# Value products as whole blocks, and where the first weights of the up-projection are kept, in a decoder layer on one core

## The chip, the cores and the metric

The kernel runs on one core of one Trainium2 chip. The metric is the device time of one execution in microseconds, the median of several runs. A profiled execution gives the trace that is read here. In what follows PE is TensorE, PEld its weight loads, DVE is VectorE, ACT is ScalarE, POOL is GpSimd, and SP is the engine that issues most of the loads; a q behind a name (SPq, POOLq) is that engine's DMA queue.

## The reference, cut to what matters

One layer of a hybrid decoder over 512 tokens of width 1024, in float32: a state-space mixer and a forgetting attention (FoX, 16 heads of 64) on the same normalised input, an output projection, and a gated MLP with a short convolution.

```
x (1, 512, 1024)

def fox_mixer(q, k, v, f_raw, ...):
    ...
    for start in range(0, s, Q_BLOCK):          # blocks of 128 queries
        ...
        p = jax.nn.softmax(jnp.where(causal, logits, -jnp.inf), axis=-1)
        outs.append(jnp.einsum('bhqk,bhkd->bhqd', p.astype(vh.dtype), vh[:, :, :end]))
...
def conv_gated_mlp(x, w_up, conv_w, conv_b, w_down):
    h = x @ w_up.astype(x.dtype)                # 1024 -> 2 x 2816
    h = causal_depthwise_conv(h, conv_w, conv_b)
    gate, val = jnp.split(h, 2, axis=-1)
    return (jax.nn.silu(gate) * val) @ w_down.astype(x.dtype)
...
    h = rms_norm(x, norm_mix_w[layer])
    ...                                         # both mixers, from one projection of h
    x = x + (mixed @ w_out[layer].astype(mixed.dtype)).astype(x.dtype)
    hf = rms_norm(x, norm_ffn_w[layer])
    x = x + conv_gated_mlp(hf, ...)
```

## The kernel before

Every large product is made in three: each operand is split into a high part (a cast to a shorter form of float32) and a low part (what the cast left), and high x high, high x low and low x high are added up in PSUM (`mm3`, L107 to L113; its matmuls all have line L110). A weight block of 128x1024 is loaded as it is, ACT casts it (`wh`), DVE subtracts (`wl`). For the up-projection this is `split_up`, L921 to L924.

The stages follow one another on PE: projections and state-space scan to about 216 us, FoX attention with further projections between its pieces to about 421, the output projection (`po`) to 438.6, the up-projection to about 650, the down-projection to the end. A scheduler writes out one order for each engine from the program's order, from priorities (`urgent()` raises what is made in it) and from marks that put one instruction behind another (`issue_after`, `keep_in_program_order`); each engine then runs its own order, and an instruction that waits holds up what stands behind it on its engine.

*FoX.* The heads go in pairs. Queries and keys of later pairs are transposed (`qkT`, L601), logits S are made (L651, L652), softmax leaves `prob`; `fox_turn` (L663 to L677) transposes `prob` in 128x128 pieces (`pT`, L674) and ACT copies them to `pt` (L676). `fox_values` (L679 to L695) multiplies by v: eight matmuls for a pair, each two records in the trace, one head in the lower 64 output rows (LO) and one in the upper (HI), alternating. In the program they keep their order, but other instructions may come between them. Products of other projections (`pw`) fill PE in this stage.

*Start of the up-projection.* w_up is cut into blocks of eleven "quads", each with four quarters B11, B12, B21, B22. Quad 0 is made plainly (`plain`, L1271 to L1287): each quarter is loaded into a `wraw` tile, split, and multiplied with the two halves of the tokens; the sums are the PSUM tiles G and Z. Its weight pairs (`wh`, `wl`) come from a spare place for B12, and otherwise from a pool `wp` of three pairs, two of which hold the output projection's last weights (`w7`) until these have been used. The tokens are normalised in four blocks `tb` (`up_norm`, L845 to L855: ACT's square L847, DVE and POOL's power L125/L126, DVE's scaling L852), transposed on PE (`hT`, L864) and split by ACT and DVE (L867 to L879) into `uh`, `ul`, `ghl`. `up_sums` (L884 to L908) makes sums of token blocks for the later quads.

Quads 1 and on take seven products, n0 to n6, instead of eight. A tile Ta is loaded with B11 (`load_a`); n0's weights are split from it; then POOL's queue adds B12 onto it by a DMA that accumulates (`more`, L967 and L968), n2's weights are split from the sum, and so on. So a later addition must wait until both splits of the step before have read Ta. The Ta tiles are one in the pool `pu` (quads 1, 4, ...) and two in the pool `ptt` (the others). SP issues the plain loads in order (L972, L978, L1277).

Of the kernel before, what the change touches and what calls it, by code (L numbers as in the profile page):

```python
# [8 lines left out]
F32 = mybir.dt.float32  # L9
F32R = mybir.dt.float32r  # L10
# [5 lines left out]
P = 128  # L16
SEQ = 512
D = 1024
NK = D // P
NTB = SEQ // P  # L20
# [13 lines left out]
LINE = 64  # L34
# [5 lines left out]
def tile_hybrid_layer(  # L40
# [18 lines left out]
    nc = tc.nc  # L59
    act, dve, pool, pe = nc.scalar, nc.vector, nc.gpsimd, nc.tensor  # L60

    cp = ctx.enter_context(tc.tile_pool(name="cp", bufs=1))
    wp = ctx.enter_context(tc.tile_pool(name="wp", bufs=2))
# [11 lines left out]
    def raw(ap):  # L75
        return ap.bitcast(F32)
# [41 lines left out]
    def mbank(name="m"):  # L118
        return bank_pools["pm"].tile([P, 512], F32, tag="m", name=name)

    def obank(name="o"):
        return bank_pools["po"].tile([P, 512], F32, tag="o", name=name)
# [9 lines left out]
    def columns(n):  # L132
        taken_columns[0] += n
        return misc[:, taken_columns[0] - n : taken_columns[0]]
# [31 lines left out]
    r = columns(NTB)  # L166
# [59 lines left out]
    for k in range(NK):  # L226
        ins = pe.matmul(pdt[:64, :], wdt[:, k, :], xh[:, k, :], start=k == 0, stop=False, skip_group_check=True)
        if k < 2:
            tc.keep_in_program_order(ins)
            keep_busy(64 * (1 - k))  # L230
        ins = pe.matmul(
            pdt[:32, :], wdt[:, k, 0:32], xl[:, k, :], start=False, stop=k == NK - 1, skip_group_check=True
        )
# [72 lines left out]
    LO, HI = slice(0, HD), slice(HD, P)  # L306
# [150 lines left out]
    squares, copied = [], {}  # L457
# [205 lines left out]
    def fox_turn(prob):  # L663
        where = {}
        for n, kbs in enumerate(((2,), (1, 3), (0,))):
            w = sum(SEQ - kb * P for kb in kbs)
            t = mbank("pT")
            pt = pf.tile([P, w], F32, tag="pt%d" % n, name="pt", bufs=4 if n == 0 else 3)
            w = 0
            for kb in kbs:  # L670
                where[kb] = (pt, w)
                for qb in range(kb, NTB):
                    o = QOFF[qb] + kb * P
                    pe.transpose(t[:, w : w + P], prob[:, o : o + P], ident)  # L674
                    w += P
            act.copy(pt, t[:, :w])  # L676
        return where  # L677

    def fox_values(pair, turned, v):  # L679
        o = obank("o")  # L680
        for kb in range(NTB):
            for i, rows in ((1, HI), (0, LO)):
                pt, w = turned[i][kb]
                ins = pe.matmul(  # L684
                    o[rows, kb * P :], v[:, kb, (2 * pair + i) % 8, :], pt[:, w : w + SEQ - kb * P],
                    start=kb == 0, stop=kb == NTB - 1, skip_group_check=True,
                )
                if (kb, i) != (0, 1):
                    tc.keep_in_program_order(ins)
        values_last.append(ins)  # L690
        mh = pmf.tile([P, SEQ], F32R, tag="mfh", name="mfh", bufs=2)
        ml = pmf.tile([P, SEQ], F32R, tag="mfl", name="mfl", bufs=2)
        act.copy(mh, o)
        dve.tensor_sub(ml, o, raw(mh))
        return mh, ml  # L695

    def urgent():
        return tc.high_priority(AHEAD)
# [37 lines left out]
    turned = {}  # L736
# [61 lines left out]
    B11, B12, B21, B22 = 0, 1, 2, 3  # L798
    ADD, SUB = ALU.add, ALU.subtract

    ptt = ctx.enter_context(tc.tile_pool(name="ptt", bufs=1, side="right", reuse_waits="tile"))
# [3 lines left out]
    pu = pu_ctx.enter_context(tc.tile_pool(name="pu", bufs=1, side="right", reuse_waits="tile"))  # L805
# [10 lines left out]
    def up_operand(n):  # L816
        return (oh[:, n], ol[:, n]) if n < 4 else (sh[:, n - 4], sl[:, n - 4])
# [16 lines left out]
    def in_turn(engine, ins):  # L834
        if engine in turn_of:
            dep = mybir.DependencyInfo(mybir.DependencyClass.NoSync, mybir.DependencyReason.DATA)
            tc.add_manual_dep(ins.ins, turn_of[engine].ins.name, dep, reason="issue_after")
        turn_of[engine] = ins
        return ins
# [44 lines left out]
    def up_sums(tb):  # L884
        s = slice((tb % 2) * P, (tb % 2 + 1) * P)
        g1, k1, g2, k2, d1, d2 = [t[:, :, s] for t in (one[:, 0], one[:, 1], two[:, 0], two[:, 1], s1, s2)]
        turn_of.update(zip(("ACT", "DVE"), made_of[tb]))

        def sum_(dst, a, b, op):
            in_turn("DVE", op(dst, a, b))  # L890

        def parts(n, src):
            h, l = [t[:, :, s] for t in up_operand(n)]
            in_turn("ACT", act.copy(h, src))
            return lambda: in_turn("DVE", dve.tensor_sub(l, src, raw(h)))

        sum_(d1, g2, k2, dve.tensor_sub)
        low3 = parts(3, d1)
        sum_(d2, d1, g1, dve.tensor_sub)
        low4 = parts(4, d2)  # L900
        low3()
        sum_(k1, k1, d2, dve.tensor_add)
        low6 = parts(6, k1)
        low4()
        sum_(g2, g1, g2, dve.tensor_sub)
        low5 = parts(5, g2)
        low6()
        low5()  # L908
# [12 lines left out]
    def split_up(r, where=None):  # L921
        h, l = where or [wp.tile([P, 1024], F32R, tag=t, name=t, bufs=3) for t in ("wh", "wl")]
        ordered(act.copy(h, r), lambda: dve.tensor_tensor(out=l, in0=r, in1=raw(h), op=SUB))  # L923
        return h, l  # L924
# [5 lines left out]
    def pair(n):  # L930
        if FROM[n] not in pairs:
            return None
        pairs[n] = pairs.pop(FROM[n])
        return pairs[n]
# [7 lines left out]
    quads = [Quad() for _ in range(NH)]  # L942
    H1, H2 = slice(0, HT), slice(HT, SEQ)

    halfway, last_product, last_pool = [None], [None], [None]

    def product(w, n, o, part, first=False, last=True):
        h, l = w
        ah, al = up_operand(n) if n is not None else (gh, gl)
        for p in range(2):  # L950
            for k in range(4):
                c = slice(p * 512 + k * P, p * 512 + (k + 1) * P)
                ins = mm3(
                    o[:, p, part], h[:, c], l[:, c], ah[:, k], al[:, k], first and k == 0, last and k == 3, grouped=False
                )
            if p == 0:
                halfway[0] = ins
        last_product[0] = ins
# [6 lines left out]
    last_more = [None]  # L965

    def more(t, quarter, q):  # L967
        last_more[0] = nc.gpsimd.dma_start(t, wup[quarter, q], accum_op=ALU.add)  # L968
# [6 lines left out]
    def load_a(q):  # L975
        u = quads[q]
        u.ta = (pu if q % 3 == 1 else ptt).tile([P, 1024], F32, tag="T", name="Ta", bufs=1 if q % 3 == 1 else 2)
        nc.sync.dma_start(u.ta, wup[B11, q])  # L978

    def n0_weights(q, where=None):  # L980
        u = quads[q]
        if not hasattr(u, "ta"):
            load_a(q)
        u.w0 = split_up(u.ta, where or pair("n0"))
        u.at = made[0] - 1
        more(u.ta, B12, q)

    def n1_weights(q):
        u = quads[q]
# [34 lines left out]
    def n0(q, where=None):  # L1024
        if not hasattr(quads[q], "w0"):
            n0_weights(q, where)
        n0_product(q)
        with urgent():
            n0_kept(q)
# [167 lines left out]
    T = []  # L1197
# [70 lines left out]
    def spare():  # L1268
        return [pa.tile([P, 1024], F32R, tag=t, name=t, bufs=1) for t in ("wh", "wl")]

    def plain(q):  # L1271
        u = quads[q]
        u.ws, u.halfway = [], []

        def weights(quarter, where=None):
            r = wp.tile([P, 1024], F32, tag="wraw", name="wraw", bufs=3)
            nc.sync.dma_start(r, wup[quarter, q])  # L1277
            u.ws.append(split_up(r, where))

        def tokens(half):  # L1280
            for n, (name, rows) in enumerate((("Z", 0), ("Z", 1), ("G", 0), ("G", 1))):
                o = getattr(u, name)
                op = ((0, 1), (None, 2))[half][rows]
                product(u.ws[n], op, o, (H1, H2)[half], rows == 0, rows == 1)
                u.halfway.append(halfway[0])

        return weights, tokens  # L1287

    for tb in range(NTB):
        if tb == 2:  # L1290
            out_part(wa1[0], m1, 1, (2, 3), rs[1])
        if tb == NTB - 1:
            weights, tokens = plain(0)
# [9 lines left out]
    quads[0].Z = two_banks("Z", "Z")  # L1303
    sum_banks.close()
    up_banks["G"] = ctx.enter_context(tc.tile_pool(name="pq", bufs=2, space=PSUM, reuse_waits="tile"))
    weights(B11)
    with urgent():
        normed = up_norm(NTB - 1)
        act.activation(warm[:, 0:1], ss[:, NTB - 1 : NTB], AF.Silu)
# [7 lines left out]
    with urgent(), tc.issue_after(quads[0].halfway[1].ins):  # L1317
        up_turn(NTB - 1, hT3)
        up_sums(NTB - 1)
    tokens(1)  # L1320
    n0(1, spare())
    n1_weights(1)
# [1 line left out]
    n2(1)  # L1324
    n5(1)
    four = [[wp.tile([P, 1024], F32R, tag=t, name=t, bufs=3) for t in ("wh", "wl")] for _ in range(3)]

    four.append([pu.tile([P, 1024 + LINE], F32R, tag=t, name=t)[:, LINE // 4 : 1024 + LINE // 4] for t in ("wh", "wl")])
    pairs.update(n2=four[0], n4=four[3], n1=four[1], n5=four[2])
    n0_weights(2)  # L1330
    n3_weights(1)
# [19 lines left out]
    q = NH - 1  # L1351
# [277 lines left out]
```

## Time and profile before

| | |
|---|---|
| median of 3 runs | 768.64 us (767.77 to 768.9) |
| profiled execution, its own time | 770.09 us |
| its span | 768.3 us |
| busy: PE / DVE / ACT / POOL | 759.0 / 600.0 / 489.0 / 201.0 us |
| granted clock of PE | 1.00 |
| DMA moved | 112.39 MB, mean 146 GB/s |

The span is shorter than the execution's own time, which has what lies around it. Rows of the time line give start, length, engine, line, operation, output<-inputs and, in brackets, how long the engine had been idle and what ended that. Rows of the chain give start, length and what ran. Matmuls are pipelined, so rows overlap; the distance between the starts of two of them says what one costs.

### The profile page before, as it was taken

The numbers are of one execution on the slowest core, as the hardware profiler recorded it, in microseconds if no ns is written. First come the engines' busy times: TensorE is split into PE (matmuls) and PEld (weight loads), VectorE is DVE, ScalarE is ACT, GpSimd is POOL, SyncE is SP. The second block draws the span as 40 slices with busy tenths as digits, with TensorE's granted clock in tenths as the row PEclk, the third lists the DMA queues.
The fourth block names the chain that finished last, engine by engine and source line by source line (L and its number), as shares of the span: only waits on it lengthen the run. The fifth ranks groups of instructions, "written<-read, shape, count | busy, mean of one in ns | idle before, by whom it ended". The sixth has DMA issues, their size and how long they took to land.

```text
span 768.3 us, 12543 instructions
## 1 busy us (share of the span) xinstructions
PE 759.0 (99%) x4647; PEld 652.2 (85%) x4647; DVE 600.0 (78%) x965; ACT 489.0 (64%) x870; POOL 201.0 (26%) x250
## 2 busy tenths in 40 slices
PE   9999999999999999999999999999999999999997
PEld 7888878888888768887777799999999999887786
DVE  5896788578567675578794887988888888998785
ACT  7655767754578667785673665666666666665461
POOL 0001013443454542314200001333333333223120
PEclk9999999999999999999999999999999999999999
DMA  9534233143155143343222318888888888589983
GB/s 341 175 105 142 84 123 121 57 137 110 57 164 165 43 137 90 116 138 110 83 83 89 106 57 162 195 196 202 195 198 196 189 194 195 144 227 204 241 180 100
DMA packets 35005, 112.39 MB, mean 146 GB/s; under 512 B 4160, under 2 KB 5248, under 8 KB 34944
## 3 DMA queue, kind: packets, MB, share of 16 engines
q1 hardware_dynamic: 24176, 74.89, 28.7%
q0 software_dynamic: 10336, 36.18, 26.2%
q8 instruction: 36, 0.59, 0.3%
q10 hardware_dynamic: 432, 0.52, 0.2%
q14 instruction: 25, 0.20, 0.1%
HBM read 105.71 MB, written 2.20 MB: 140 GB/s over the span
## 4 chain that ended last, share of the span: by engine, by line
PE 92%; issue 3%; DMA 1%; POOL 1%; DVE 1%; ACT 0%; DVEq 0%; POOLq 0%; ACTq 0%
PE G L110 19%; PE pw L110 17%; PE g L110 13%; PE po L110 12%; PE Z L110 10%; PE Y L110 3%; PE o L684 3%; PE X L110 2%; PE pT L674 2%; PE y L501 2%; DMA T<-in_wdown_dram 1%; PE j L110 1%; PE S L652 1%; PE S L651 1%; POOL T L1207 1%
## 5 line engine op out<-in xcount | busy, mean ns | idle before, releaser
L110 PE MATMUL pw<-wl,xh 128*128 128x512 f32 x192 | 75.9, 395 | 0.0
L110 PE MATMUL pw<-wh,xh 128*128 128x512 f32 x192 | 75.3, 397 | 0.0
L110 PE MATMUL pw<-wh,xl 128*128 128x512 f32 x192 | 75.3, 394 | 0.0
L110 PE MATMUL G<-uh,wh 128*128 128x256 f32 x264 | 72.6, 277 | 0.4 <-ACT wh L923 0.4
L110 PE MATMUL G<-uh,wl 128*128 128x256 f32 x264 | 71.6, 277 | 1.1 <-DVE wl L923 1.1
L110 PE MATMUL G<-ul,wh 128*128 128x256 f32 x264 | 72.5, 276 | 0.0
L97 DVE TENSOR_TENSOR wl<-wraw,wh 128x1024 fp32r<-128x1024 f32 x51 | 63.2, 1241 | 9.3 <-ACT wh L96 9.1
L96 ACT CAST wh<-wraw 128x1024 fp32r<-128x1024 f32 x51 | 53.9, 1056 | 14.7 <-PE g L110 5.3
L110 PE MATMUL g<-xl,wh 128*128 128x512 f32 x144 | 56.7, 394 | 0.0
L110 PE MATMUL g<-xh,wh 128*128 128x512 f32 x144 | 56.5, 393 | 0.0
L110 PE MATMUL g<-xh,wl 128*128 128x512 f32 x144 | 56.5, 393 | 0.0
L968 POOL DMA_DIRECT2D Ta<-in_wup_dram x30 | 26.2, 873 | 113.1 <-DVE wl L923 113.1
L1218 ACT CAST wh<-T 128x1024 fp32r<-128x1024 f32 (+1 forms) x32 | 31.5, 985 | 35.5 <-DMA T<-in_wdown_dram 19.2
L657 ACT ACTIVATE prob<-prob,nm 128x128 f32<-128x128 f32 (+1 forms) x64 | 35.8, 561 | 25.9 <-DVE nm L653 25.8
L923 DVE TENSOR_TENSOR wl<-Ta,wh 128x1024 fp32r<-128x1024 f32 x40 | 48.7, 1218 | 2.6 <-ACT wh L923 2.6
L653 DVE CUSTOM_DVE_ANT_0 prob<-S,prob 128x128 f32<-128x128 f32 (+1 forms) x64 | 30.1, 487 | 26.3 <-PE S L652 23.8
L110 PEld LDWEIGHTS G<-uh,wh 128*128 128x128 f32 x264 | 49.6, 188 | 0.8 <-ACT wh L923 0.8
L110 PEld LDWEIGHTS G<-uh,wl 128*128 128x128 f32 x264 | 48.9, 188 | 1.3 <-DVE wl L923 1.3
L110 PEld LDWEIGHTS G<-ul,wh 128*128 128x128 f32 x264 | 49.6, 188 | 0.0
L1218 DVE TENSOR_TENSOR wl<-T,wh 128x1024 fp32r<-128x1024 f32 (+1 forms) x32 | 36.5, 1139 | 14.8 <-ACT wh L1218 14.6
L923 ACT CAST wh<-Ta 128x1024 fp32r<-128x1024 f32 x40 | 42.1, 1052 | 6.2 <-DMA Ta<-in_wup_dram 4.2
L110 PE MATMUL G<-sh,wh 128*128 128x256 f32 x160 | 44.2, 276 | 0.0
(296 smaller groups left out, 2416.9 us busy)
## 6 DMA issues: line engine op xcount, KB each, us to landing
Ta<-in_wup_dram POOLq DMA_DIRECT2D x30, 512.0 KB, 5.4
T<-in_wdown_dram POOLq DMA_DIRECT2D x20, 512.0 KB, 7.3
wraw<-in_wqk_dram SPq DMA_DIRECT2D x16, 512.0 KB, 3.6
wraw<-in_wout_dram SPq DMA_DIRECT2D x16, 512.0 KB, 3.4
wraw<-in_wup_dram SPq DMA_DIRECT2D x14, 512.0 KB, 4.5
wraw<-in_wxbc_dram SPq DMA_DIRECT2D x11, 512.0 KB, 3.4
Ta<-in_wup_dram SPq DMA_DIRECT2D x10, 512.0 KB, 6.8
Tb<-in_wup_dram SPq DMA_DIRECT2D x10, 512.0 KB, 6.4
```

Source lines behind the costliest of these rows:

```text
L96: act.copy(h, r)
L97: dve.tensor_tensor(out=l, in0=r, in1=raw(h), op=ALU.subtract)
L110: ins = pe.matmul(o, a, b, start=start and n == 0, stop=stop and n == 2, **kw)
L501: ins = pe.matmul(o[rows, j * P : (j + 1) * P], w[:, h * HD : (h + 1) * HD], m[:, h, :], start=start and j == 0, stop=stop and j == 3, ski ...
L651: pe.matmul(sps[:, :n], qst, ks[:, 0, :n], start=True, stop=False)
L653: dve.tensor_tensor_reduce(out=p, in0=sps[:, :n], in1=p, scale=-1.0, scalar=-NEG, op0=ALU.add, op1=ALU.min, accum_out=nm[:, qb : qb + 1],)
L657: act.activation(p, p, AF.Exp, scale=-1.0, bias=nm[:, qb : qb + 1], accum_out=sm[:, qb : qb + 1])
L674: pe.transpose(t[:, w : w + P], prob[:, o : o + P], ident)
L684: ins = pe.matmul(o[rows, kb * P :], v[:, kb, (2 * pair + i) % 8, :], pt[:, w : w + SEQ - kb * P], start=kb == 0, stop=kb == NTB - 1, skip ...
L923: ordered(act.copy(h, r), lambda: dve.tensor_tensor(out=l, in0=r, in1=raw(h), op=SUB))
L968: last_more[0] = nc.gpsimd.dma_start(t, wup[quarter, q], accum_op=ALU.add)
L1218: ordered(act.copy(hs, src[:, :n]), lambda: dve.tensor_tensor(out=ls, in0=src[:, :n], in1=raw(hs), op=SUB))
```

## The change

Three things are done.

1. `fox_values` makes its matmuls at raised priority, and the first of them stands behind the last copy of both heads' `pt`. `fox_turn` returns that copy.
2. Quad 0's quarters B11 and B21 are loaded into the two T tiles of `ptt`, which hold Ta of quads 2 and 3 later. B11's pair of high and low part is put at the far end of `pu` (`far_pair`), a place that was already used later for n4's pair. The product of B11 with the first half of the tokens is made by `low_last`: all eight high x high, then the eight with the weight's low part, then the eight with the tokens' low part.
3. Quad 1's n0 weights are split from a tile of their own, T0, with a second load of B11. Ta gets its B11 and the addition of B12 before that, behind the norm of the last token block.

```
     def fox_values(pair, turned, v):
         o = obank("o")
+        dep = mybir.DependencyInfo(mybir.DependencyClass.Sync, mybir.DependencyReason.DATA)
+        with urgent():
+            for kb in range(NTB):
+                for i, rows in ((1, HI), (0, LO)):
+                    pt, w = turned[i][0][kb]
...
+                    if (kb, i) != (0, 1):
+                        tc.keep_in_program_order(ins)
+                    else:
+                        for t in turned:
+                            tc.add_manual_dep(ins.ins, t[1].ins.name, dep, reason="issue_after")
...
+    def low_last(w, n, o, part):
+        (h, l), (ah, al) = w, up_operand(n)
+        for a, b in ((h, ah), (l, ah), (h, al)):
+            for p in range(2):
+                for k in range(4):
+                    c = slice(p * 512 + k * P, p * 512 + (k + 1) * P)
+                    last_product[0] = halfway[0] = pe.matmul(
+                        o[:, p, part], a[:, c], b[:, k], start=a is h and b is ah and k == 0, stop=False, skip_group_check=True
+                    )
...
-        u.w0 = split_up(u.ta, where or pair("n0"))
+        u.w0 = split_up(u.ta if where is None else u.t0, where or pair("n0"))
         u.at = made[0] - 1
-        more(u.ta, B12, q)
+        if where is None:
+            more(u.ta, B12, q)
...
+    def far_pair():
+        return [pu.tile([P, 1024 + LINE], F32R, tag=t, name=t)[:, LINE // 4 : 1024 + LINE // 4] for t in ("wh", "wl")]
...
+        held = {n: load_rows(n, ptt, "T", 2) for n in (B11, B21)}
         def weights(quarter, where=None):
-            r = wp.tile([P, 1024], F32, tag="wraw", name="wraw", bufs=3)
-            nc.sync.dma_start(r, wup[quarter, q])
+            r = held[quarter] if quarter in held else load_rows(quarter, wp, "wraw", 3)
             u.ws.append(split_up(r, where))
...
+                if half == 0 and n == 2:
+                    low_last(u.ws[n], op, o, H1)
+                else:
+                    product(u.ws[n], op, o, (H1, H2)[half], rows == 0, rows == 1)
...
-    weights(B11)
+    weights(B11, far_pair())
...
+    load_a(1)
+    more(quads[1].ta, B12, 1)
+    dep = mybir.DependencyInfo(mybir.DependencyClass.Sync, mybir.DependencyReason.DATA)
+    tc.add_manual_dep(last_more[0].ins, normed.ins.name, dep, reason="issue_after")
+    quads[1].t0 = ptt.tile([P, 1024], F32, tag="T", name="T0", bufs=2)
+    nc.sync.dma_start(quads[1].t0, wup[B11, 1])
     tokens(1)
     n0(1, spare())
```

On PE at pair 1 of FoX (281 us in the trace of before), `o<-pt,v` are the value products (L684 before, L687 now), `qkT` and `pT` transposes, `pw` the filling projection; rows with - are before, with + now:

```order
 L110 MATMUL pw<-wh,xl 128x512
 L110 MATMUL pw<-wh,xh 128x512
-L684 MATMUL o<-pt,v 64x512
+L687 MATMUL o<-pt,v 64x512 x2
+L687 MATMUL o<-pt,v 64x384 x2
+L687 MATMUL o<-pt,v 64x256 x2
+L687 MATMUL o<-pt,v 64x128 x2
+L601 MATMUL qkT<-ident,tok 128x128 x5
+L674 MATMUL pT<-ident,prob 128x128 x2
 L601 MATMUL qkT<-ident,tok 128x128
-L684 MATMUL o<-pt,v 64x512
-L601 MATMUL qkT<-ident,tok 128x128
```

The eight matmuls now stand one behind the other, with the transposes behind them; the block starts at the same place in PE's order.

On ACT at the start of the up-projection (430 to 441 us), `x_85` is the layer's input to the norm, L847 the square of a token block, `wh<-wraw` a cast of quad 0's weights, `uh` and `one` the first two token blocks. Before:

```order
L847 ACTIVATE xw,misc<-x_85 128x1024 x2
L923 CAST wh<-wraw 128x1024 x2
L867 CAST uh<-hT 128x8x128
L868 COPY one<-hT 128x8x128
L867 CAST uh<-hT 128x8x128
L868 COPY one<-hT 128x8x128
L847 ACTIVATE xw,misc<-x_85 128x1024
L923 CAST wh<-wraw 128x1024 x2
L847 ACTIVATE xw,misc<-x_85 128x1024
L1309 ACT_TABLE_LOAD
```

and now, where the square is L853, the casts L929, and `wh<-T` are the casts of B11 and then B21:

```order
L853 ACTIVATE xw,misc<-x_85 128x1024 x2
L929 CAST wh<-wraw 128x1024 x2
L929 CAST wh<-T 128x1024
L873 CAST uh<-hT 128x8x128
L874 COPY one<-hT 128x8x128
L873 CAST uh<-hT 128x8x128
L874 COPY one<-hT 128x8x128
L929 CAST wh<-T 128x1024
L853 ACTIVATE xw,misc<-x_85 128x1024 x2
L1341 ACT_TABLE_LOAD
```

B11's cast has moved from behind the third square to ahead of the token operands, and B21's from behind that square to ahead of it.

On SP, the loads of the up-projection's start; `T` are B11 and B21 of quad 0, `T_4621` is T0, Ta and Tb tiles of the later quads. Before:

```order
L1277 DMA wraw<-in_wup_dram 128x1024 x3
L978 DMA Ta<-in_wup_dram 128x1024 x3
L1277 DMA wraw<-in_wup_dram 128x1024
L972 DMA wraw<-in_wup_dram 128x1024
L972 DMA Tb<-in_wup_dram 128x1024 x2
L972 DMA wraw<-in_wup_dram 128x1024 x2
```

and now:

```order
L1299 DMA wraw<-in_wup_dram 128x1024 x2
L989 DMA wraw<-in_wup_dram 128x1024
L1299 DMA T<-in_wup_dram 128x1024 x2
L995 DMA Ta<-in_wup_dram 128x1024
L989 DMA Tb<-in_wup_dram 128x1024 x2
L1358 DMA T_4621<-in_wup_dram 128x1024
L995 DMA Ta<-in_wup_dram 128x1024 x2
L989 DMA wraw<-in_wup_dram 128x1024 x2
```

Ta of quads 2 and 3 has moved behind T0, and there is one load more.

More of the change, by code (lines that the diff above doesn't have):

```diff
@@ L675, in fox_turn @@
                     w += P
-            act.copy(pt, t[:, :w])
-        return where
+            copied = act.copy(pt, t[:, :w])
+        return where, copied
     def fox_values(pair, turned, v):
         o = obank("o")
[L681 to L689, printed above, removed]
+        dep = mybir.DependencyInfo(mybir.DependencyClass.Sync, mybir.DependencyReason.DATA)
[3 more added lines that the diff above has]
+                    pt, w = turned[i][0][kb]
+                    ins = pe.matmul(
+                        o[rows, kb * P :], v[:, kb, (2 * pair + i) % 8, :], pt[:, w : w + SEQ - kb * P],
+                        start=kb == 0, stop=kb == NTB - 1, skip_group_check=True,
+                    )
[4 more added lines that the diff above has]
+                            tc.add_manual_dep(ins.ins, t[1].ins.name, dep, reason="issue_after")
         values_last.append(ins)
@@ L945, in tile_hybrid_layer @@
     halfway, last_product, last_pool = [None], [None], [None]
+    def low_last(w, n, o, part):
[6 more added lines that the diff above has]
+                        o[:, p, part], a[:, c], b[:, k], start=a is h and b is ah and k == 0, stop=False, skip_group_check=True
+                    )
     def product(w, n, o, part, first=False, last=True):
@@ L1273, in plain, with load_rows @@
         u.ws, u.halfway = [], []
+        def load_rows(quarter, pool_, tag, bufs):
+            r = pool_.tile([P, 1024], F32, tag=tag, name=tag, bufs=bufs)
+            nc.sync.dma_start(r, wup[quarter, q])
+            return r
+        held = {n: load_rows(n, ptt, "T", 2) for n in (B11, B21)}
         def weights(quarter, where=None):
-            r = wp.tile([P, 1024], F32, tag="wraw", name="wraw", bufs=3)
-            nc.sync.dma_start(r, wup[quarter, q])
+            r = held[quarter] if quarter in held else load_rows(quarter, wp, "wraw", 3)
             u.ws.append(split_up(r, where))
@@ L1283, in tokens @@
                 op = ((0, 1), (None, 2))[half][rows]
-                product(u.ws[n], op, o, (H1, H2)[half], rows == 0, rows == 1)
+                if half == 0 and n == 2:
+                    low_last(u.ws[n], op, o, H1)
+                else:
+                    product(u.ws[n], op, o, (H1, H2)[half], rows == 0, rows == 1)
                 u.halfway.append(halfway[0])
@@ L1326, in tile_hybrid_layer @@
     four = [[wp.tile([P, 1024], F32R, tag=t, name=t, bufs=3) for t in ("wh", "wl")] for _ in range(3)]
-    four.append([pu.tile([P, 1024 + LINE], F32R, tag=t, name=t)[:, LINE // 4 : 1024 + LINE // 4] for t in ("wh", "wl")])
+    four.append(far_pair())
     pairs.update(n2=four[0], n4=four[3], n1=four[1], n5=four[2])
```

## The prediction

> **What bounds the kernel now.** I read the totals of the page first, then its chain, then the list of what TensorE waited for, and after that the time line at the three places that the change touches.
>
> ```profile
> span 768.3 us, 12543 instructions
> PE 759.0 (99%) x4647; PEld 652.2 (85%) x4647; DVE 600.0 (78%) x965; ACT 489.0 (64%) x870; POOL 201.0 (26%) x250
> PE 92%; issue 3%; DMA 1%; POOL 1%; DVE 1%; ACT 0%; DVEq 0%; POOLq 0%; ACTq 0%
> ...
> PE G L110 <- DVE wl L923: 1.1, 1, 1.1
> ...
> PE G L110 <- ACT wh L923: 0.4, 1, 0.4
> ```
>
> TensorE (PE) works 759.0 of 768.3 us and carries 92% of the chain. So there are two ways only to gain: less TensorE time for the same products, or one of its few waits taken away. Two of these waits, 1.1 and 0.4 us, stand at the first products of the up-projection, where the change puts its new tiles. A gain reaches the end only if what follows has its inputs early enough to move with it.
>
> The profiled execution took 770.09 us with a span of 768.3; the median of the runs shown is 768.64, 1.45 less. I subtract microseconds saved from the median.
>
> **Part one: a pair's value products as a block.** Seven of the eight pairs stand as blocks already. Pair 1, at 281 us, does not: key transposes (qkT) stand between its matmuls. The chain of waits shows both forms.
>
> ```profile
> 281.25 1.00 PE o L684 x2
> 282.25 0.26 PE qkT L601
> 282.51 1.00 PE o L684 x2
> 283.51 0.26 PE qkT L601
> 283.77 0.79 PE o L684 x2
> ...
> 284.82 0.79 PE o L684 x2
> ...
> 285.87 0.80 PE o L684 x8
> ...
> 287.91 4.12 PE pw L110 x18
> ...
> 307.32 2.31 PE o L684 x16
> 309.62 1.02 PE qkT L601 x8
> ...
> 310.88 0.22 PE pT L674 x2
> ...
> 311.34 0.44 PE pT L674 x4
> ```
>
> The same 16 value records cost 1.00+1.00+0.79+0.79+0.80 = 4.38 us when cut up, and 2.31 in a block: 2.07 saved. A qkT between them costs 0.26, in a row of eight 1.02/8 = 0.13. Whole: pair 1 with eight qkT and six pT runs from 281.25 to 287.91, 6.66 us; the same pieces in block form are 2.31+1.02+0.22+0.44 = 3.99. The difference is 2.67 us, all on TensorE. [...]
>
> What might take it back: the block waits for both heads' last copy of pT, which ScalarE finishes well ahead, and the softmax of the next pairs must follow.
>
> ```profile
> 276.36 0.62 ACT L676 COPY pt<-pT 128x512 f32<-128x512 f32 x1
> ...
> 340.89 0.29 DVE L653 CUSTOM_DVE_ANT_0 prob<-S,prob 128x128 f32<-128x128 f32 x1 [0.99 <-PE S L652]
> ...
> 339.91 0.59 ACT L676 COPY pt<-pT 128x512 f32<-128x512 f32 x1 [0.92 <-PE pT L674]
> ```
>
> The copy ends at 276.98, 4.3 us before the block, so the new wait costs nothing. At 340 VectorE (DVE) and ScalarE (ACT) had each been idle almost a microsecond, waiting for TensorE: there they can come 0.9 us earlier at once, and the remainder has to be found in the idle time of the pairs before. I expect a little to be lost on the way: 2.4 us kept, between 1.0 (only those idle 0.9 us pass on) and 2.67.
>
> **Part two: the first quad's weights.** Time line of TensorE between out-projection (po) and the MLP's first sums (G), and of the engines that feed it:
>
> ```profile
> 438.32 0.39 PE L110 MATMUL po<-wh,mfl 128*128 128x512 f32 x1
> 439.06 0.39 PE L110 MATMUL G<-uh,wh 128*128 128x256 f32 x1 [0.35 <-ACT wh L923]
> 439.29 0.28 PE L110 MATMUL G<-ul,wh 128*128 128x256 f32 x1
> 440.62 0.38 PE L110 MATMUL G<-uh,wl 128*128 128x256 f32 x1 [1.06 <-DVE wl L923]
> ...
> 443.34 0.28 PE L110 MATMUL G<-ul,wh 128*128 128x256 f32 x1
> 443.45 0.60 PE L864 MATMUL hT<-ident,xw 128*128 128x128 f32 x4
> ...
> 431.55 1.06 ACT L923 CAST wh<-wraw 128x1024 fp32r<-128x1024 f32 x1 [0.31 <-PE po L110]
> ...
> 436.80 1.22 DVE L869 TENSOR_TENSOR ul<-one,uh 128x1024 fp32r<-128x1024 f32 x1
> 436.92 1.06 ACT L847 ACTIVATE xw<-x 128x1024 f32<-128x1024 f32 x1 [0.67 <-DVE x L278]
> 437.98 1.98 ACT L923 CAST wh<-wraw 128x1024 fp32r<-128x1024 f32 x2
> 439.35 1.22 DVE L923 TENSOR_TENSOR wl<-wraw,wh 128x1024 fp32r<-128x1024 f32 x1
> 440.49 1.41 DVE L852 SCALAR_TENSOR_TENSOR xw<-x,misc,nw 128x512 f32<-128x512 f32 x2
> ```
>
> Out-projection matmuls stand 0.23 apart, so TensorE is free at 438.55. The 26 G matmuls in front of hT stand 0.113 apart when nothing is late (170.00 us for 1500 in the quads, quoted below), 2.95 us. Unhindered, hT would start at 441.50; it starts at 443.45. The loss is 1.95 us, and its cause is B11's cast at 437.98 and its low part at 439.35 to 440.57.
>
> With the change B11's cast stands right behind the one of 431.55, so at about 432.6 to 433.6, and its low part, behind another of 1.22 on VectorE, is ready near 435.5. Products then start at 438.55. The last eight of the first product need token block 1's low operand (ul). It was ready at 438.02; now B11's cast on ScalarE and its low part on VectorE stand ahead of it, so I put it 1.2 to 1.6 later, 439.6 at most. The eight come at 438.55+16x0.113 = 440.36. That order (high, weight-low, operand-low) leaves 0.7 us.
>
> What is late next is hT itself. B21's cast now stands ahead of the square of token block 2 (L847) on ScalarE: before, that square began at 436.92, and the cast can't begin before its pair is released, which I put some five out-projection matmuls before the last, 438.55-5x0.23 = 437.4. So the square begins at about 438.5 and ends 439.6; 0.2 of reading the sum, VectorE's and POOL's small steps and the first half of L852 (0.7) give xw near 441.8. TensorE comes at 441.50: 0.3 us of wait remain. The gain is 1.95-0.35 = 1.6. Bounds: 1.95 if hT is ready in time; 0.5 if B21's pair is freed only after the last out-projection matmul, 438.55, which puts the square 1.1 us later. I take 1.6, since in the trace both casts could run at 437.98, before 438.55.
>
> **Part three: a tile of its own for quad 1's first block.** Its worth is that part two doesn't come back as a wait 20 us later.
>
> ```profile
> 458.88 0.95 POOL L968 DMA_DIRECT2D Ta<-in_wup_dram  x1 [16.30 <-DVE wl L923]
> ...
> 464.38 1.05 ACT L923 CAST wh<-Ta 128x1024 fp32r<-128x1024 f32 x1 [2.28 <-DMA Ta<-in_wup_dram]
> 465.46 1.23 DVE L923 TENSOR_TENSOR wl<-Ta,wh 128x1024 fp32r<-128x1024 f32 x1 [1.17 <-ACT wh L923]
> ...
> 467.20 0.28 PE L110 MATMUL Z<-uh,wh 128*128 128x256 f32 x1
> Ta<-in_wup_dram POOLq DMA_DIRECT2D x7, 512.0 KB, 5.6
> Ta<-in_wup_dram SPq DMA_DIRECT2D x4, 512.0 KB, 4.5
> ```
>
> Before, Ta gets B12 added on only after its first use, at 458.88; the cast waits for it to land at 464.38, the low part is ready at 466.69, and its product starts at 467.20. Some 0.5 us of slack: moved 1.6 earlier, TensorE would wait 1.1 there. With T0 the addition goes out after the norm of block 3, one turn of some 2 us behind block 2's end at 442.4, so near 444.6; it lands 5.6 later at about 450, and the low part is ready long before 465. Cost: one more load of 512 KB, 4.5 us on queues, and SP's next two Ta loads wait for tiles, the second until T0's low part is read, about 458.6; it is quad 3's, more than the 19 us of a quad (7 products of 24 matmuls) away. Behind it in SP's queue stand two loads of wraw for later products of quad 1; they would land by about 465, and I see no product that needs them before 470. I cost this part at 0, between 0 and +1.1 (the addition isn't there in time).
>
> **Whether the rest follows.** From 480 to 650 TensorE does nothing but matmuls, one after another:
>
> ```profile
> 453.20:461.75 8.55, 8.55 (x75) 1.00 0.16 19
> 480.00:650.00 170.00, 170.00 (x1500) 1.00 0.86 194
> ```
>
> (Window, its length, TensorE's busy time with count, granted clock, DMA share, GB/s.) 1500 matmuls in 170.00 us without a gap: the loop is not held by transfers, and a start 4 us earlier passes to the end. DMA is 0.86 busy but fed by the same loop.
>
> **Sum**: 2.4 + 1.6 + 0 = 4.0 us; 768.64 - 4.0 = 764.6.
>
> **Rivals.**
> - *The value block gives, the up start doesn't.* ScalarE's queue is the bound there, in which each of these operations takes 1.0 us. If the square of block 2 is late by 1.1 more, only 0.5 of part two is left, and if 0.3 is also missed in part one, 768.64-2.1-0.5 = 766.0. For it speaks that B21's cast must wait for a pair; against it, that even there ScalarE idles 0.67 us for VectorE, by the row at 436.92.
> - *The value block's gain is eaten by softmax.* Only 1.0 of 2.67 gets through, with 1.6 above: 766.0; if both rivals hold, 768.64-1.0-0.5 = 767.1. Against it: at 340 both engines wait for TensorE, not it for them.
> - *Slower: tiles in other places run matmuls at another pace.* Between 453.20 and 461.75 matmuls stand 8.55/72 = 0.119 apart (by start times; the window counts 75 with its edges), against 0.113, with a granted clock of 1.00 and DMA at 0.16, so there is a 5% that no row explains. T0, the T tiles and the far pair move high and low parts to other places; if the 1500 matmuls of the loop took that pace, they would cost 1500x0.006 = 9 us, and the time would be 773.6. It decides from 4.0/1500 = 2.7 ns per matmul. Against it: the same kinds of tiles rotate through the loop in any case. [...]
> - *The new tiles aren't free in time* (T's loads late, or the far pair held): part two gives 0 and B11 is as late as before: 768.64-2.4 = 766.2.
>
> **Chances.** 764.6, both gains almost whole: 0.58. Up start largely lost or tiles late, about 766: 0.15. FoX partly eaten, about 766, of which a third with both: 0.12. A loss elsewhere that cancels it, within 0.2%: 0.07. Slower: 0.08. A run of this kernel tells 0.2% (1.54 us) from no change, so 767.10 and below is faster: 0.58+0.15+0.08 = 0.81; same 0.11; slower 0.08. The low end is both bounds whole, 768.64-2.67-1.95 = 764.0, less 0.9 for the spread of the runs (767.77 against 768.64); the high end the doubly reduced case, 767.1.
>
> **What would show it.** Part one: 16 value records in one row near 281, 2.3 us long, and the next pw 2.6 earlier. Part two: G begins without a wait at the last po's end plus 0.23, and hT 3 to 3.4 us after it, with a wait of a few tenths for DVE's xw. Part three: n2's cast waits for no transfer. Wrong I would be if the loop's 1500 matmuls took other than 170 us, if hT waited over 1 us, or if pair 2's or 3's S came no earlier than before.

## The result and the profile after

The changed kernel takes 764.07 us (763.39 to 765.09, 4 runs) against 768.26 of the kernel before: ratio 0.9945, 95% interval 0.9933 to 0.9958, so 4.2 us less. The forecast was 764.6. In the traces the value products gave 0.3 and the up start 0.2 more than their terms.

Totals of the page after, and then the list of TensorE's waits (total, times, longest):

```profile
span 762.3 us, 12540 instructions
PE 755.4 (99%) x4647; PEld 651.7 (85%) x4647; DVE 599.7 (79%) x965; ACT 488.4 (64%) x870; POOL 203.0 (27%) x250
```

```profile
PE g L219 <- DVE misc L141: 1.0, 1, 1.0
PE X L110 <- DVE wl L1236: 1.0, 2, 0.8
PE po L110 <- DVE x L278: 0.3, 1, 0.3
PE g L231 <- DVE xl L194: 0.2, 1, 0.2
```

The two waits for G's weights are gone from the list, and TensorE works 3.6 us less for the same 4647 matmuls. Of this, 2.7 us are at pair 1, by the chain there (start, length, what ran); the rest is 0.3 at the up-projection's start and some 0.5 elsewhere, most of it in the down-projection.

```profile
281.45 2.30 PE o L687 x16
283.75 0.70 PE qkT L601 x5
...
285.43 4.36 PE pw L110 x19
```

The 16 value records now take 2.30 us instead of 4.38, and the first pw stands at 285.43 instead of 287.91. The changed kernel was 0.20 late at the block's start (281.45 against 281.25), so pair 1 gave 2.68.

The start of the up-projection, on PE, then ACT, then DVE:

```profile
435.83 0.39 PE L110 MATMUL po<-wh,mfl 128*128 128x512 f32 x1
436.06 1.10 PE L960 MATMUL G<-uh,wh 128*128 128x256 f32 x8
437.00 1.11 PE L960 MATMUL G<-uh,wl 128*128 128x256 f32 x8
437.94 1.10 PE L960 MATMUL G<-ul,wh 128*128 128x256 f32 x8
...
439.00 0.28 PE L110 MATMUL G<-ul,wh 128*128 128x256 f32 x1
439.22 0.63 PE L870 MATMUL hT<-ident,xw 128*128 128x128 f32 x4
...
430.02 1.04 ACT L929 CAST wh<-T 128x1024 fp32r<-128x1024 f32 x1
...
435.89 1.06 ACT L853 ACTIVATE xw<-x 128x1024 f32<-128x1024 f32 x1
...
431.71 1.22 DVE L929 TENSOR_TENSOR wl<-T,wh 128x1024 fp32r<-128x1024 f32 x1
...
438.32 1.42 DVE L858 SCALAR_TENSOR_TENSOR xw<-x,misc,nw 128x512 f32<-128x512 f32 x2 [0.66 <-POOL misc L126]
```

G begins 0.23 after the last po matmul, without a wait; B11's low part is ready at 432.93, 4 us before its first use. hT starts 3.16 after G; before it was 4.39. The last G matmul starts at 439.00, so hT could have come at 439.11: 0.1 us of wait is left, by the rows for DVE's xw, whose first half ends at about 439.0. Last po to hT shrank from 5.13 to 3.39, by 1.74.

From there to the loop's end both kernels do the same in the same time. One piece of the chain near 647 us, before and after:

```profile
649.61 2.73 PE Y L110 x12
```

```profile
645.32 2.73 PE Y L110 x12
```

Here the change stands at -4.29 us, and with the 0.20 that this execution was late from its start, at -4.49 (2.68 at pair 1, 1.74 at the up start, 0.07 over the 206 us between).

The two spans differ by 6.0, though. The remaining 1.7 us arise behind this row, in the down-projection, which the change doesn't touch: from the row to the end it is 118.69 us before and 116.99 after. That stage differs between executions: in the profiles of the experiments below, whose last stage is the same code, it takes 116.6 to 118.0. And the profiled execution of the kernel before took 770.09 us where the median is 768.26. I take the medians' 4.2 and the 4.5 of the part that both do alike; they agree within the interval of the ratio, which is 3.2 to 5.1 us.

### The profile page after: what moved, and what is told of

It reads as the page before. It is cut to its first block, busy times and chain, and to the rows that moved or that the text cites. A ratio compares the mean times of both kernels' runs of the same rounds, so it can differ in the third digit from the quotient of the medians.

```text
span 762.3 us, 12540 instructions
## 1 busy us (share of the span) xinstructions
PE 755.4 (99%) x4647; PEld 651.7 (85%) x4647; DVE 599.7 (79%) x965; ACT 488.4 (64%) x870; POOL 203.0 (27%) x250
## 4 chain that ended last, share of the span: by engine, by line
PE 88%; issue 4%; DMA 3%; DVE 3%; POOL 1%; ACT 0%; SPq 0%; DVEq 0%; POOLq 0%; ACTq 0%
PE G L110 19%; PE pw L110 17%; PE g L110 13%; PE po L110 12%; PE Z L110 11%; PE o L687 2%; DMA T<-in_wdown_dram 2%; PE pT L674 2%; PE Y L110 2%; PE y L501 2%; PE j L110 1%; PE S L652 1%; PE S L651 1%; POOL T L1225 1%; PE qkT L601 1%
## 5 line engine op out<-in xcount | busy, mean ns | idle before, releaser
L110 PE MATMUL G<-uh,wh 128*128 128x256 f32 x256 | 70.3, 276 | 0.0
L110 PE MATMUL G<-ul,wh 128*128 128x256 f32 x256 | 70.3, 276 | 0.0
L110 PE MATMUL G<-uh,wl 128*128 128x256 f32 x256 | 69.2, 276 | 0.0
L929 DVE TENSOR_TENSOR wl<-Ta,wh 128x1024 fp32r<-128x1024 f32 x39 | 47.4, 1216 | 0.6 <-ACT wh L929 0.6
L110 PE MATMUL G<-sl,wh 128*128 128x256 f32 x160 | 44.2, 276 | 0.0
```

The costliest lines, as they stand in the source:

```text
L110: ins = pe.matmul(o, a, b, start=start and n == 0, stop=stop and n == 2, **kw)
```

## Experiments

**The two halves alone.** The value products as a block, everything else as before; and the reverse. (Both are the diff of the change, cut in two.)

> Only the value products as a block; the up-projection's start as in the kernel before. My theory: the two gains are independent, so this one gives 2.7 us at pair 1 and keeps 2.5 of them to the end: ratio to before 0.9967, with the first G still waiting 1.1 and 0.4 us for its weights. Rival: the weights' casts do not move with TensorE, so an earlier out-projection only makes the first G wait longer; then 1 us or less remains (0.999).

> Only the weights' places and quad 1's T0; the value products as before, cut up at pair 1. My theory: 1.7 to 1.8 us less than before (ratio 0.9977), hT 3.1 to 3.2 us after the first G, no wait at the first G. Rival: the gain at the start needs the earlier value products (less queued on ScalarE and VectorE by then), so less than 1 us.

Measured: values alone 765.74 us, ratio 0.9965 (0.9953 to 0.9977); start alone 766.29, ratio 0.9978 (0.9964 to 0.9993). By the ratios that is 2.7 and 1.7 us, in sum 4.4 against 4.2 for both; by the medians, against 768.51 of the kernel before measured beside them, 2.8 and 2.2. The two differ for start alone because one of its twelve runs took 771.78, of a kind that comes up below, and a median hardly sees one run. Its trace gives the same as the changed kernel's: last po (437.97) to hT (441.36) takes 3.39. In values alone, TensorE still waits where it did before:

```profile
436.34 0.39 PE L110 MATMUL G<-uh,wh 128*128 128x256 f32 x1 [0.35 <-ACT wh L929]
436.56 0.28 PE L110 MATMUL G<-ul,wh 128*128 128x256 f32 x1
437.90 0.38 PE L110 MATMUL G<-uh,wl 128*128 128x256 f32 x1 [1.05 <-DVE wl L929]
```

The wait did not grow though TensorE came 2.7 us earlier (last po at 435.60 instead of 438.32), so the weights' casts move with TensorE: they wait for a pair that TensorE sets free. The gains are independent, and both rivals fall.

**Why the block is cheaper.** In the block, matmuls for the upper and the lower 64 rows alternate. This kernel puts the four of one head ahead of the four of the other:

```
-            for kb in range(NTB):
-                for i, rows in ((1, HI), (0, LO)):
+            for i, rows in ((1, HI), (0, LO)):
+                for kb in range(NTB):
```

> The change, but each pair's value products stand as the four of one head and then the four of the other, so that neighbours use the same half of the array. Theory A, overlap of neighbours in different halves: each block then costs about the 4.4 us of the cut-up pair instead of 2.3, and with 8 pairs the time is some 16 us above the changed kernel. Theory B, the cut-up pair lost its time at changes between half and whole width alone: the block stays near 2.3 us and the time is unchanged.

Measured: 777.15 us, ratio 1.0127 (1.0098 to 1.0156), 13 us above the changed kernel. Chain at pair 1:

```profile
283.74 2.30 PE o L687 x8
286.14 1.46 PE o L687 x6
```

The block now runs from 283.74 to 287.60 (two short records are in neither row), so 3.9 us instead of 2.30, 1.6 more, and for eight pairs 12.5 of the 13. So theory B falls: two neighbours in different halves run side by side, and that is worth most of the 2.07 us. The size was off, because I took the cut-up pair's 4.38 as a form without any overlap. It isn't one: its last four matmuls alternate and take 0.80, and only its first four (eight records, 1.00+1.00+0.79+0.79 = 3.58) stand alone. The trace of the kernel before gives the parts: a record of 512 columns lasts 0.64 us and two of the same half 1.07, so the second starts 0.43 behind the first; with 384 columns it is 0.54 and 0.86, so 0.32. Those eight would take 3.01 with nothing between them, and in the changed kernel's block they take 1.55 (281.38 to 282.93). So, as an estimate from these rows, the overlap gives 1.5 us, and 0.6 of the 3.58 is what four pieces cost more with a full-width transpose behind each (1.00 instead of 2x0.43, 0.79 instead of 2x0.32). The transposes themselves gain 0.6 (0.26 against 0.13 each). Why either costs more beside the other is not shown.

**What in part two does it.** Three kernels undo one piece each: the far pair (`weights(B11)` instead of `weights(B11, far_pair())`), the raw tiles (`held = {}`), the order in the first product (`low_last` never used).

> The change, but B11's high and low part go into a pair of the common pool again, which the out-projection's last weights hold. My theory: this is the whole of part two, so 1.6 to 1.8 us come back, with the first G waiting for B11's cast and low part (0.3 to 0.5 and 0.8 to 1.1 us). Rival: the raw tiles do it (B11 and B21 loaded earlier), and less than 0.5 comes back.

> The change, but B11 and B21 of quad 0 are loaded into the usual raw tiles instead of T tiles. My theory: they are worth nothing, since a raw tile is free for B11 at once and for B21 once B12 is split, 4 us before its cast: 0.0 us against the changed kernel (within 0.3). Rival: B21's load, or the loads for quad 1 that it pushes back, come late, and 0.5 to 2 us are lost at the square of block 2 or at n1's weights.

> The change with the first product in the usual order (each high x high followed by low parts). My theory: token block 1's low operand, ready 0.9 us after the first G in the changed kernel, now holds the second matmul; TensorE waits 0.9 us there, and hT comes 0.8 later, since 0.1 of wait ahead of hT goes. Time 0.8 above the changed kernel. Rival: hT is bound by VectorE's normalised rows, not by the products, and nothing is lost (0.0 to 0.1).

Without the far pair: 766.10 us, ratio 0.9963 (0.9951 to 0.9976). The time line shows both waits again:

```profile
436.10 0.39 PE L110 MATMUL po<-wh,mfl 128*128 128x512 f32 x1
436.83 1.19 PE L960 MATMUL G<-uh,wh 128*128 128x256 f32 x8 [0.35 <-ACT wh L929]
438.40 1.19 PE L960 MATMUL G<-uh,wl 128*128 128x256 f32 x8 [0.38 <-DVE wl L929]
...
440.56 0.60 PE L870 MATMUL hT<-ident,xw 128*128 128x128 f32 x4
```

Last po to hT takes 4.46 us, 1.07 more than with it. (The medians differ by 2.0, but this profile's last stage is 1.1 us longer than the changed kernel's, and that is the spread spoken of above.) My 1.6 to 1.8 was too much: the new order of the first product needs the low part eight matmuls later and hides some 0.7 of its lateness even here.

Without the raw tiles: 764.12 us; last po (436.27) to hT (439.66) takes 3.39 as in the changed kernel. As expected, they are worth nothing.

Without the order, the second matmul waits for the tokens' low part:

```profile
435.97 0.28 PE L110 MATMUL G<-uh,wh 128*128 128x256 f32 x1
436.97 0.39 PE L110 MATMUL G<-ul,wh 128*128 128x256 f32 x1 [0.72 <-DVE ul L875]
```

At the first Z product and up to 490 us that kernel stands 0.8 us behind the changed one, as expected. Its time, 765.92, doesn't measure this (0.9946 to 0.9990), for a reason that comes below. So part two is the far pair (1.1 when it is taken away) and the order (0.8). Last po to hT is 5.13 us with neither, 4.46 with the order alone, 4.19 with the far pair alone (435.75 to 439.93) and 3.39 with both: the two nearly add.

**Part three.** T0 removed, n0's weights from Ta, B12 added after them:

```
-        u.w0 = split_up(u.ta if where is None else u.t0, where or pair("n0"))
+        u.w0 = split_up(u.ta, where or pair("n0"))
         u.at = made[0] - 1
-        if where is None:
-            more(u.ta, B12, q)
+        more(u.ta, B12, q)
...
-    load_a(1)
-    more(quads[1].ta, B12, 1)
...
-    nc.sync.dma_start(quads[1].t0, wup[B11, 1])
```

> The change without its third part: no T0, n0's weights from Ta and B12 added only after that. My theory: the wait that part two would push on comes back at the first product of n2 of quad 1, 1.1 to 1.2 us of TensorE waiting, and the time is 1.1 us above the changed kernel (0.9960 of before instead of 0.9945). Rival: the addition lands early enough in any case, 0.0 us of wait, and T0 is worth nothing.

Measured: 770.81 us, ratio 1.0046 (1.0020 to 1.0072): slower than before, and by the medians 6.7 us above the changed kernel, not 1.1. Eight of its twelve runs took 768.4 to 771.3 us and four took 775.3 to 778.1; the profiled one, 769.57, is of the eight and 5.5 above the changed kernel's. Its POOL queue, ACT, PE, and three windows (window, length, TensorE's busy time with count, granted clock, DMA share, GB/s):

```profile
455.02 0.94 POOL L985 DMA_DIRECT2D Ta<-in_wup_dram  x1 [14.54 <-issue]
...
463.88 1.04 ACT L929 CAST wh<-Ta 128x1024 fp32r<-128x1024 f32 x1 [6.23 <-DMA Ta<-in_wup_dram]
...
464.98 0.45 PE L110 MATMUL Z<-uh,wh 128*128 128x256 f32 x1 [1.84 <-ACT wh L929]
465.22 0.42 PE L110 MATMUL Z<-ul,wh 128*128 128x256 f32 x1
466.24 0.58 PE L110 MATMUL Z<-uh,wl 128*128 128x256 f32 x1 [0.60 <-DVE wl L929]
```

```profile
462.90:465.10 2.20, 0.36 (x4) 1.00 0.00 0
465.20:471.90 6.70, 6.10 (x28) 0.50 0.59 94
472.00:475.00 3.00, 3.00 (x28) 1.00 0.68 134
```

Two things that my 1.1 lacked. The addition took 8.8 us to land, not the 5.6 that I had carried over. A load of wraw by SP went out 0.6 us behind it; in the changed kernel, where a load of SP's went out 0.5 us behind the first addition, that one took 8.3. That the load is the reason fits both, but wasn't tested by itself. And behind the wait of 1.84 us the granted clock fell to 0.50 for 6.8 us, in which matmuls stand 0.213 us apart instead of 0.113. The wait of 0.60 us came after the fall, so it isn't part of its cause. In all, 2.4 us of wait cost 5.9. By the windows the fall came between 465.10 and 465.20, some 2.3 us after the last quick matmul had started (462.86), and behind an idle time of 1.84 us; how short an idle time still does this is not shown. In the changed kernel the addition went out early and the cast waits for no transfer:

```profile
442.57 0.94 POOL L985 DMA_DIRECT2D Ta<-in_wup_dram  x1 [2.15 <-DVE xw L858]
...
455.52 1.05 ACT L929 CAST wh<-Ta 128x1024 fp32r<-128x1024 f32 x1 [0.43 <-PE Z L110]
```

**The kernel before once more**, for the last stage:

> The kernel before once more, for the spread of its last stage. In the two profiles shown the down-projection is 1.6 us shorter after the change, which no step of mine accounts for. Theory: that is spread between executions (the last stage hangs on transfers), so the profile of this run has a last stage that differs from the first profile's by about 1 us, and its span is some 766.5. Rival: the change shortened it, and this profile repeats the first one's last stage within 0.3 us.

Measured: 769.02 us; its span, 768.4, and its last stage repeat the first profile's within 0.1 us. That is the rival's outcome, so the spread isn't seen between these two. But both profiled executions (770.09 and 770.13) were slower than their kernel's medians, 768.26 and 769.02. The changed code, on the other hand, has last stages from 0.4 us shorter to 1.1 longer than the profile shown (no raw tiles; no far pair). None of its profiles reaches the 118.7 of the two before, so a small part of the 1.7 may belong to the change; the medians, whose 4.2 is less than the 4.5 of the part in front, don't show it. What sets that stage stays open.

**A slower pace in some executions.** The kernel without the order had a profile of 769.3 us span. Windows of it:

```profile
470.00:492.00 22.00, 22.00 (x197) 1.00 0.86 185
494.00:642.00 148.00, 148.00 (x1258) 1.00 0.83 186
```

148.00 us for 1258 matmuls are 117.6 ns each, where the changed kernel's profile has 113.2 (160.00 us for 1414 from 484 to 644), with a clock of 1.00 in both. The slow part begins behind a wait of 0.1 us at 496 and lasts to the loop's end. Four more kernels asked whether the changed kernel has this, and whether such a wait is its cause. The last three put one more subtraction ahead of one low part:

```
+            if late:
+                dve.tensor_tensor(out=l[:, 0:256], in0=r[:, 0:256], in1=raw(h)[:, 0:256], op=SUB)
             return dve.tensor_tensor(out=l, in0=r, in1=raw(h), op=SUB)
```

> The changed kernel once more. In the profile of the kernel without the special order, a wait of 0.1 us at 496 us was followed by 1270 matmuls at 117.8 ns instead of 113.3, and some executions of that kernel, of the one without T tiles and of the start alone were 5 to 6 us above their fastest. Theory P: this belongs to the weights' new places, which leave less time in the first quads, so the changed kernel has it too, in about 1 of 6 executions (some 769 to 770 us). Theory Q: it belongs to those variants alone, and all executions stay within 763 to 766 us.

> The changed kernel with one extra VectorE subtraction of 256 columns (about 0.35 us) ahead of one low part in quad 2, whose product starts within 0.02 us of it; nothing else moves. Theory P: TensorE waits about 0.3 us near 492 us and all matmuls of the quads behind it, some 1350, stand 117.8 ns apart instead of 113.3: 6 us more. Theory Q: the slow pace came from something else, and the wait costs itself, 0.3 us.

> The same extra subtraction four quads later, near 568 us. Theory P: the wait of 0.3 us and half as many matmuls at the slow pace, some 680: 3 us more. Theory Q: 0.3 us.

> As the first of these, with an extra subtraction of 1024 columns (about 1.1 us) at the same place. Theory P: 1.1 us of wait and 6 us of slow pace. Theory Q: 1.1 us. A third outcome, the wait without the slow pace here but with it for the short one, would mean that not every wait changes the pace.

The changed kernel again: 763.86 us (762.71 to 771.11, 12 runs), ratio 0.9958 (0.9935 to 0.9982). Three of the twelve took 769.8 to 771.1, the others 762.7 to 765.1, so it has it too, as theory P said. Its profile was one of the three:

```profile
479.01 1.05 ACT L929 CAST wh<-Ta 128x1024 fp32r<-128x1024 f32 x1 [1.00 <-DMA Ta<-in_wup_dram]
...
481.24 0.69 DVE L1108 TENSOR_TENSOR Z<-z,G 128x512 f32<-128x512 f32 x1
...
481.83 0.28 PE L110 MATMUL G<-ul,wh 128*128 128x256 f32 x1
481.98 0.39 PE L110 MATMUL G<-uh,wh 128*128 128x256 f32 x1
```

```profile
484.00:644.00 160.00, 160.00 (x1361) 1.00 0.84 190
```

An addition lands 1.0 us late for ACT; DVE, 0.7 late behind it, finishes reading G at 481.93; TensorE's next matmul into G starts at 481.98, 0.04 late, and from there on matmuls stand 117.6 ns apart.

The three kernels with the extra subtraction (764.02, 763.18 and 763.88 us) don't answer the second question: in none of them did TensorE wait there, since I had misread which product takes that low part; DVE's slack was more than 1 us. But the last one met the late addition by itself, with a wait twice as long (0.08 us), and kept the quick pace:

```profile
482.47 0.28 PE L110 MATMUL G<-ul,wh 128*128 128x256 f32 x1
482.66 0.39 PE L110 MATMUL G<-uh,wh 128*128 128x256 f32 x1
```

```profile
484.00:640.00 156.00, 156.00 (x1378) 1.00 0.87 197
```

So the slow pace twice began right behind a short wait, and another short wait at the same place was not followed by it; nor was a wait of 0.1 us at 484 in start alone. That the wait causes it is not shown.

The other runs on record tie the pace to the new start of the up-projection, as theory P does. Of the 84 executions of the kernel before none is more than 2.6 us above the median of its session, and of the six with the value block alone none is even 1 us above theirs. Of all kernels with the new start or most of it, 14 of 84 executions lie 5 to 9 us above the median of the rest of their kernel. That all of these are the slow pace is an inference, since only two of them were profiled. They came without the raw tiles, without the order and without T0 too; without the far pair none came, but in five runs, too few to tell. Which piece brings it stays open.

## Why the prediction was right, point by point

**Value products, -2.4 forecast, -2.7 measured.** The 2.67 from the chain's rows was right. Of the rows' 2.07 the overlap gives 1.5, by the estimate above, since the pair's last four matmuls had overlapped already; the other 0.6 is what the pieces cost more with a transpose behind each. The step that failed is the allowance of 0.3 for the softmax behind it: at 350 us the kernel with this part alone stands 2.7 earlier, the whole of it. DVE and ACT had been waiting for TensorE there, as the rows at 340 said.

**Up start, -1.6 forecast, -1.7 measured at hT and -1.8 at the loop's end.** Each step was seen: G without a wait, hT 3.16 us after G (3 to 3.4 forecast), hT held by DVE's xw. I had 0.3 of wait left there and 0.1 is left; the square began at 435.89 in a kernel that is 2.5 us earlier, 0.1 ahead of the 438.5 that I had put, and what follows it was 0.1 shorter. Another 0.1 went the other way: the first 24 G matmuls stand 118 ns apart, 2.82 us in all, not the 113 that I had taken from the loop.

**T0 and the early addition, 0 forecast, 0 measured, but its price when missing was mis-sized**: +1.1 forecast, 5.5 measured between the profiles and 6.7 between the medians, by the addition's 8.8 us to land and the clock's fall. In the changed kernel, too, the addition landed in 8.3 us instead of 5.6, at 450.9; its cast comes 4.6 us later, so this did no harm. The change without its third part was slower than the kernel before. I had looked for the slow rival in the wrong place.

**Rivals.** Neither gain was eaten. The new tiles were free in time; the T tiles would not even have been needed. The slower pace, to which I gave a small chance as a property of the tiles' places, exists, but as something that comes in some executions: 3 of 16 of the changed kernel, each 6 us longer than the rest. In the first four runs there was none, by chance. The median of all 16 is 763.96, but their mean is 765.1 against 768.6 of the 84 executions of the kernel before, so on average the change saves some 3.5 us.

**Time.** 764.07 lies in 763.1 to 767.1, and 0.5 below the forecast. Most of this 0.5 is the kernel before itself: with a fourth run its median is 768.26, not the 768.64 that I subtracted from, so the medians give 4.2 us against 4.0. The traces give 4.5, 0.3 more from the first term and 0.2 from the second. Which of the two is nearer, the spread of the runs doesn't tell.

## What to carry to other kernels

Here a pair of half-width matmuls paid off only while the two halves were neighbours: transposes put between them, or one half after the other, gave back most of what the overlap is worth (2.30 us in alternation, 3.9 by halves, 4.38 cut up). When TensorE is moved earlier, look at the next transfer that was just in time, and price its lateness with what the clock does behind the wait, not with the wait alone (without T0, 2.4 us of wait cost 5.9). And when one change holds several pieces, undo them one by one: here one tile was worth some 6 us, one pair 1.1, one order 0.8, and one relocation nothing.

## What the runs showed of the hardware that I had not expected

Behind a wait of 1.84 us the granted clock fell to 0.50 for 6.8 us; behind the wait of 1.1 us in the kernel before, two matmuls after one of 0.4 us, it stayed at 1.00 (438 to 450 us). The same matmul stream ran at 113 or at 118 ns per matmul with a granted clock of 1.00, and could stay at the slower pace for 1300 matmuls, 6 us; the profile's clock doesn't show it, only the distance of the rows does. Of the 40 DMAs that accumulate 512 KB onto Ta and Tb in the changed kernel's trace, 24 landed in 5.2 to 5.7 us and 16 in 6.2 to 8.6. The first, with a load of SP's 0.5 us behind it, took 8.3, and nine with such a load 0.8 us behind took 7.2 to 8.6; in the kernel without T0 one with a load 0.6 us behind took 8.8.
